# A convolution with max pooling: first quarter loaded as fp32, cleared tiles on GpSimd, a new order of all instructions

## The chip, the cores and the metric

One core of a Trainium2 chip runs the kernel. The metric is the device time of one execution in microseconds; before the change its median is 99.69 us over three runs (99.55 to 99.73).

## The reference

```python
x_pad = np.pad(x, ((0, 0), (0, 0), (1, 1), (1, 1)))
conv[b, co] += weight[co, ci, kh, kw] * x_pad[b, ci, kh:kh+h, kw:kw+w]   # over ci, kh, kw
output[b, c, i, j] = np.max(conv[b, c, 2*i:2*i+2, 2*j:2*j+2])
```

`x` is 16 x 64 x 64 x 64 and `weight` 128 x 64 x 3 x 3, both fp32; the output is 16 x 128 x 32 x 32. So it is a 3x3 convolution with padding 1 and a 2x2 maximum.

## The kernel before

**Tiling.** Two images of 64 channels fill the 128 partitions: eight pairs p. A pair is cut into four quarters q of 16 image rows, that is R = 8 output rows of 64 columns before column pooling. Such a quarter is a *step*; there are 32, numbered in the order of `SEQ`, and steps 0, 1, 2, 3 are the quarters of pair 0. Lane l (0 or 1) is one image of the pair. A matmul of a step uses 64 partitions of one lane, contracts the channels and writes 128 output channels x 512 (8 rows x 64) into one PSUM bank; matmuls of the two row halves of the array run side by side. Three matmuls (kw = 1, 0, 2) make a *product*.

**The arithmetic in the rows.** For an output pair of rows, with input rows r0 to r3 and kernel rows g0, g1, g2, a W step keeps four row tiles: E = r1 - r2, S = r1 + r2, and V, which holds both r2 - r0 (Ve) and r3 - r1 (Vo). Its products are P2 (block GM on E), P0 (G0 on V), P3 (G2 on V) and P1 (GP on S), with GM and GP half of g0 + g2 -/+ g1. A K step multiplies input rows themselves: PAa (D2 = g2 - g1), PAb (G0), PBa (D0 = g0 - g1), PBb (G2), and PR (G1 on the tile KS = r1 + r2). Step 0 is a K step, step 1 a W step. In step 0 each product but PR is cut into parts a and b of four rows: `PAb.0.1b` is step 0, lane 1, part b.

**The weights.** SP loads `wraw` (L182). DVE, ACT and POOL form the blocks G0, G1, G2, D0, D2, then GM and GP from `gsum` (tokens `c.g0`, `c.D2`, `c.GS` and so on, L211 to L231); PE transposes a block (three transposes, token T, L252), and ACT or DVE copies it from PSUM to `wt` (token TV, L263 and L267).

**The input.** SP loads the first 9 rows of pair 0 as fp32 into `first` (L184), and the tokens XO and XE cast its odd and even rows into `rows_x` (L214). All other rows come by GpSimd's DMA queue with a cast to bf16 under way (`load`, L180), in the order of `LOADS`; the first `EARLY` = 3 are issued ahead of everything else, the others at their LH tokens. DVE clears `zeros` and the top and bottom edge rows of `rows_x` (L190, L191). `make_identity` builds `ident` on POOL. Eight matmuls on constants run first on PE (L466).

**After the products.** ACT copies A's bank out (EV) and copies A into B's bank as a seed (SE, L415); DVE takes the row maximum into the bank (MX, L427), then the column maximum, alone (RM, L436) or with ACT's copy of the odd columns (OD, L431; CM, L448). SP stores (ST, ST2).

**The order.** `ORDER` is a hand-kept list of tokens, executed from left to right; the suffix names the engine (v DVE, a ACT, g POOL) or the PSUM bank. Each engine runs its own tokens in that order, and semaphores connect them. A row operation on POOL also waits for DVE's last row operation or cast ahead of it in the list (`behind`):

```python
def row_op(e, out, in0, in1, op):
    inst = eng[e].tensor_tensor(out=out, in0=in0, in1=in1, op=op)
    if e == "g":
        behind(inst, last_row[0])
    else:
        last_row[0] = inst
```

Of the kernel before, what the change touches and what calls it, by code (L numbers as in the profile page):

```python
# [17 lines left out]
XO.0a:v T.D0:4 XE.0a:a PAa.0.0a:0 PAa.0.1a:5 c.GS:g PAa.0.0a PAa.0.1a PAa.0.0a PAa.0.1a TV.D0:v PAb.0.0a  # L18
PAb.0.1a PAb.0.0a PAb.0.1a PAb.0.0a PAb.0.1a TV.G2:v PAa.0.0b PAa.0.1b PAa.0.0b PAa.0.1b LH.8 PAa.0.0b
PAa.0.1b c.GM:v PAb.0.0b PAb.0.1b PAb.0.0b PAb.0.1b PAb.0.0b PAb.0.1b PBa.0.0a:2 PBa.0.1a:4 PBa.0.0a  # L20
PBa.0.1a KS.0:v EV.0.1 PBa.0.0a PBa.0.1a PBb.0.0a PBa.0.1b PBb.0.0a PBa.0.1b TV.G1:v PBb.0.0a PBa.0.1b
T.GM:1 EV.0.0 c.GP:v PBb.0.1a PBa.0.0b PBb.0.1a PBa.0.0b PBb.0.1a PBa.0.0b TV.GM:a PBb.0.1b PBb.0.0b LH.9
E.1:v PBb.0.1b PBb.0.0b PBb.0.1b PBb.0.0b T.GP:0 P2.1.1:3 P2.1.0:1 MX.0.0 S.1:g TV.GP:a P2.1.1 P2.1.0 P2.1.1
P2.1.0 MX.0.1 PR.0.0 SE.1.1:5 PAa.2.1:0 PR.0.0 LH.10 PAa.2.1 PR.0.0 V.1:v SE.1.0:6 PAa.2.1 PAa.2.0:7 PR.0.1
PAa.2.0 RM.0.0 PR.0.1 PAa.2.0 PR.0.1 PAb.2.0 P0.1.1 PAb.2.0 E.3:v OD.0.1 P0.1.1 PAb.2.0 P0.1.1 P0.1.0 CM.0.1
P3.1.1 P0.1.0 EV.1.1 P3.1.1 P0.1.0 V.3:v P3.1.1 P3.1.0 P2.3.1:4 P3.1.0 EV.1.0 P2.3.1 P3.1.0 MX.1.1 KS.2:g
P2.3.1 P2.3.0:3 EV.2.0 PAb.2.1 P2.3.0 PAb.2.1 MX.1.0 P2.3.0 PAb.2.1 PBa.2.0:1 P1.1.1 SE.3.0:7 PBa.2.0 Ve.4:v
P1.1.1 PBa.2.0 P1.1.1 PBb.2.0 S.3:v EV.2.1 PBa.2.1:2 PBb.2.0 E2.4:v PBa.2.1 PBb.2.0 OD.1.1 PBa.2.1 P1.1.0
SE.3.1:0 PBb.2.1 P1.1.0 CM.1.1 PBb.2.1 P1.1.0 Vo.4:g PBb.2.1 P0.3.0 MX.2.0 P0.3.1 OD.1.0 P0.3.0 P0.3.1
P0.3.0 CM.1.0 P0.3.1 P3.3.0 P3.3.1 EV.3.0 P3.3.0 MX.2.1 S2.4:g ST2.1 P3.3.1 P3.3.0 P3.3.1 PR.2.0 EV.3.1  # L30
P2.4.1:6 PR.2.0 MX.3.0 P2.4.1 PR.2.0 P2.4.1 P2.4.0:3 PR.2.1 OD.2.0 P2.4.0 MX.3.1 PR.2.1 P2.4.0 PR.2.1 P1.3.0
CM.2.0 PAa.6.1:5 P1.3.0 PAa.6.1 KS.6:g P1.3.0 RM.2.1 PAa.6.1 PAa.7.0:1 P1.3.1 OD.3.0 PAa.7.0 P1.3.1 PAa.7.0
SE.4.0:4 CM.3.0 P1.3.1 PAb.7.0 PAb.6.1 PAb.7.0 LH.11 V.5:v OD.3.1 PAb.6.1 PAb.7.0 PAb.6.1 P0.4.0 SE.4.1:7
PAa.7.1:2 P0.4.0 CM.3.1 PAa.7.1 P0.4.0 PAa.7.1 P3.4.0 ST2.3 V2.8:v P0.4.1 EV.4.0 P3.4.0 P0.4.1 P3.4.0 P0.4.1
P2.5.0:0 EV.7.0 P3.4.1 P2.5.0 P3.4.1 P2.5.0 EV.4.1 MX.4.0 P3.4.1 PAa.6.0:3 E.8:g PAb.7.1 PAa.6.0 SE.5.0:1
PAb.7.1 PAa.6.0 MX.4.1 PAb.7.1 PAb.6.0 PBa.7.1:6 PAb.6.0 EV.7.1 PBa.7.1 PAb.6.0 S2.8:v LH.12 PBa.7.1 P1.4.0
P1.4.1 P1.4.0 EV.6.0 V2.10:v P1.4.1 P1.4.0 P1.4.1 PBa.6.0:2 PBb.7.1 OD.4.0 PBa.6.0 PBb.7.1 PBa.6.0 OD.4.1
# [515 lines left out]
```

## Time and profile before

| | |
|---|---|
| median of three runs | 99.69 us |
| the profiled execution | 99.57 us, span 97.8 us |
| TensorE clock granted | 0.996 |
| first product of step 0 | 5.55 us |
| step 1 begins on PE | 9.38 us |
| PE busy | 92.4 us, 845 matmuls |
| DVE busy | 88.9 us |
| ACT busy | 82.9 us |
| POOL busy | 68.4 us |

Times within the profile count from the span's start. A row of a timeline gives the start, the duration, engine, line, operation, out<-in with partitions x elements, how many instructions are merged, and in brackets the idle time ahead with what ended it. PE is matmuls, PEld weight loads, DVE VectorE, ACT ScalarE, POOL GpSimd, SP the engine that issues most stores. Landing is the time from a DMA's issue to its completion.

### The profile page before, as it was taken

The page shows a single profiled execution, that of the slowest core. Times are in us where ns is not written, and L with a number is a line of the kernel's source. Part 1 is how long each engine was busy: PE and PEld are TensorE (multiplying, and loading weights), DVE is VectorE, ACT ScalarE, POOL GpSimd, SP SyncE. Part 2 cuts the span into 40 slices and gives each one's busy share as a digit, 9 for nine tenths or more (in the row PEclk, how much of TensorE's full clock was granted, in tenths as well). Part 3 has the DMA queues.
Part 4 walks back from the last instruction along what each step waited for, and adds up shares of the span by engine and source line. Part 5 has one row for each costly group of instructions (what it writes and reads, how often), then busy time and mean ns, then how long its engine had stood idle before and what let it go on. Part 6 is the DMA issues. An engine that isn't in the chain of part 4 may idle for free.

```text
span 97.8 us, 2315 instructions
## 1 busy us (share of the span) xinstructions
PE 92.4 (94%) x845; PEld 57.6 (59%) x845; DVE 88.9 (91%) x172; ACT 82.9 (85%) x177; POOL 68.4 (70%) x60
## 2 busy tenths in 40 slices
PE   6998999999999999999999999999999999999920
PEld 2394554555886885666667555564555557777600
DVE  3459999999999999999999999999998999997960
ACT  5466688599779999999999999999989999889830
POOL 5994545936488867989584876759499779599200
PEclk9999999999999999999999999999999999999998
DMA  2999999999999999999999740405050503254052
GB/s 55 237 145 196 169 204 216 218 233 230 250 225 244 225 245 330 238 227 299 225 230 291 285 144 27 188 3 189 32 214 0 217 4 137 84 214 144 17 188 80
DMA packets 7675, 17.36 MB, mean 178 GB/s; under 512 B 624, under 2 KB 2544, under 8 KB 7024
## 3 DMA queue, kind: packets, MB, share of 16 engines
q0 software_dynamic: 2160, 8.24, 43.3%
q1 hardware_dynamic: 5216, 8.72, 25.6%
q10 hardware_dynamic: 288, 0.26, 0.8%
q8 instruction: 6, 0.10, 0.4%
q14 instruction: 5, 0.04, 0.1%
HBM read 17.07 MB, written 8.39 MB: 260 GB/s over the span
## 4 chain that ended last, share of the span: by engine, by line
PE 83%; POOL 5%; DVE 4%; issue 3%; ACT 1%; ACTq 0%; POOLq 0%
PE acc L369 82%; POOL rows_x L180 4%; DVE o L448 2%; DVE acc L427 1%; POOL gsum L219 1%; ACT acc L415 1%; PE acc L252 1%; DVE wq L219 1%; ACT ev L401 1%; POOL ident masks.py:199 0%; POOL ident masks.py:197 0%; ACTq L415 0%; POOLq L534 0%
## 5 line engine op out<-in xcount | busy, mean ns | idle before, releaser
L369 PEld LDWEIGHTS <-wt 64*128 64x128 bf16 x816 | 55.2, 94 | 31.2 <-issue 1.8
L369 PE MATMUL acc<-wv,wt 64*128 64x504 bf16 (+1 forms) x264 | 49.9, 377 | 0.0
L427 DVE TENSOR_TENSOR acc<-acc,ev 128x512 f32<-128x512 f32 x64 | 42.7, 689 | 1.2 <-ACT acc L415 0.5
L369 PE MATMUL acc<-ws,wt 64*128 64x512 bf16 (+1 forms) x168 | 40.8, 376 | 0.0
L369 PE MATMUL acc<-we,wt 64*128 64x512 bf16 (+1 forms) x168 | 39.3, 377 | 0.0
L401 ACT ACTIVATE ev<-acc 128x512 f32<-128x512 f32 x56 | 32.7, 605 | 1.8 <-PE acc L369 1.7
L415 ACT COPY acc<-acc 128x512 f32<-128x512 f32 x56 | 32.2, 590 | 2.1 <-PE acc L369 1.3
L219 POOL TENSOR_TENSOR ws<-rows_x 128x512 bf16<-128x512 bf16 (+1 forms) x12 | 17.6, 1477 | 4.2 <-DVE wv L219 1.9
L431 ACT COPY od<-acc 128x256 f32<-128x256 f32 x49 | 18.0, 379 | 2.8 <-PE acc L369 2.3
L219 POOL TENSOR_TENSOR we<-rows_x 128x512 bf16<-128x512 bf16 (+1 forms) x10 | 15.4, 1542 | 6.3 <-DVE wv L219 3.8
L448 DVE TENSOR_TENSOR o<-acc,od 128x256 f32<-128x256 f32 (+1 forms) x48 | 19.1, 420 | 0.1
L369 PE MATMUL acc<-rows_x,wt 64*128 64x504 bf16 (+7 forms) x120 | 16.5, 332 | 0.0
L219 POOL TENSOR_TENSOR wv<-rows_x 128x1024 bf16<-128x1024 bf16 (+1 forms) x6 | 14.7, 2449 | 2.3 <-DVE ws L219 1.6
L369 PE MATMUL acc<-vh,wt 64*128 64x504 bf16 (+1 forms) x72 | 16.0, 377 | 0.0
L219 POOL TENSOR_TENSOR vh<-rows_x 128x512 bf16<-128x512 bf16 x8 | 9.2, 1155 | 5.6 <-DVE we L219 3.1
L436 DVE TENSOR_REDUCE o<-acc 128x256 f32<-128x512 f32 x15 | 10.2, 680 | 0.0
L180 POOL DMA_DIRECT2D rows_x<-in_x_dram x15 | 8.6, 575 | 2.1 <-DMA rows_x<-in_x_dram 1.3
L219 DVE TENSOR_TENSOR wv<-rows_x 128x1024 bf16<-128x1024 bf16 (+1 forms) x11 | 9.8, 891 | 0.0
L369 PE MATMUL acc<-ks,wt 64*128 64x504 bf16 (+1 forms) x24 | 6.0, 376 | 0.0
L403 ACT COPY ev<-acc 128x512 f32<-128x512 f32 x8 | 4.5, 586 | 0.9 <-PE acc L369 0.9
L219 DVE TENSOR_TENSOR we<-rows_x 128x1024 bf16<-128x1024 bf16 (+1 forms) x9 | 5.1, 564 | 0.0
L219 DVE TENSOR_TENSOR ws<-rows_x 128x512 bf16<-128x512 bf16 (+1 forms) x8 | 4.7, 588 | 0.0
(26 smaller groups left out, 24.1 us busy)
## 6 DMA issues: line engine op xcount, KB each, us to landing
out_dram<-o SPq DMA_DIRECT2D x13, 512.0 KB, 6.5
rows_x<-in_x_dram POOLq DMA_DIRECT2D x5, 1024.0 KB, 13.5
rows_x<-in_x_dram POOLq DMA_DIRECT2D x4, 256.0 KB, 8.4
out_dram<-o SPq DMA_DIRECT2D x3, 256.0 KB, 2.9
rows_x<-in_x_dram POOLq DMA_DIRECT2D x1, 528.0 KB, 11.9
out_dram<-o SPq DMA_DIRECT2D x4, 128.0 KB, 2.0
rows_x<-in_x_dram POOLq DMA_DIRECT2D x1, 496.0 KB, 12.7
rows_x<-in_x_dram POOLq DMA_DIRECT2D x2, 240.0 KB, 9.1
```

What stands on the lines that cost most here:

```text
L180: nc.gpsimd.dma_start(out=xs[p][:, lo + 1 : hi + 1, :], in_=rows_of(p, lo, hi))
L219: inst = eng[e].tensor_tensor(out=out, in0=in0, in1=in1, op=op)
L252: nc.tensor.transpose(tp[:, (j - lo) * 128 : (j - lo + 1) * 128], wq[:, BLOCKS[m]].rearrange("a i j c -> a (i j c)")[:, (j - lo) * CI : (j ...
L369: yield lambda kw=kw, o0=o0, o1=o1, c0=c0, c1=c1: nc.tensor.matmul(acc[t][:, i0:i1, o0:o1], wt[l * CI : l * CI + CI, K * BLOCKS[block] + T ...
L401: nc.scalar.mul(t, acc[bank["A", s, l]], -1.0)
L403: nc.scalar.copy(out=t, in_=acc[bank["A", s, l]])
L415: nc.scalar.copy(out=acc[b], in_=acc[bank["A", s, l]])
L427: nc.vector.tensor_tensor(out=t, in0=t, in1=lanes(ev[s], l), op=MAX)
L431: nc.scalar.copy(out=t[:, l], in_=sums(s, l)[..., 1::2])
L436: nc.vector.tensor_reduce(out=lanes(outs(s), l), in_=pairs, axis=mybir.AxisListType.X, op=MAX,)
L448: nc.vector.tensor_tensor(out=t, in0=a[..., 0::2], in1=u, op=MAX)
```

## The change

`first` now holds the whole first quarter with one row more (17 rows), in two transfers from SP; the load of rows 9 to 16 by GpSimd's queue is gone, and no load is issued ahead of `make_identity`. The two clears go from DVE to POOL. In step 0 the products of the plain blocks, PAb and PBb, open the PSUM groups instead of PAa and PBa (`TAPS_FIRST`). XO and XE exist for both parts now. `ORDER` is new from the first token to the last. (The file also gains two functions, `sums_begin` and `sums_end`, that no token of the new list calls.)

```diff
-LOADS = ((0, 9, 17), (0, 17, 33), (0, 33, 49), (0, 49, 64), (1, 0, 17), ...
-EARLY = 3
+LOADS = ((0, 17, 33), (0, 33, 49), (0, 49, 64), (1, 0, 17), ...
+EARLY = 0
+TAPS_FIRST = 1
 ORDER = """
-LH.3 LH.4 c.g0:a c.D2:v LH.5 c.g2:v c.g1:a T.D2:0 T.G0:1 LH.6 c.D0:v TV.D2:a T.G2:2 T.G1:3 TV.G0:a LH.7
+LH.0 c.g0:a c.g2:v c.D2:g c.g1:v T.G2:0 c.D0:v T.G0:1 TV.G2:a T.G1:2 LH.1 T.D2:3 XE.0a:a TV.G0:v LH.2 T.D0:0
...
-    first = const.tile([128, R + 1, W], FP32, name="first")
-    nc.sync.dma_start(out=first, in_=rows_of(0, 0, R + 1))
+    first = const.tile([128, 2 * R + 1, W], FP32, name="first")
+    for lo, hi in ((0, R + 1), (R + 1, 2 * R + 1)):
+        nc.sync.dma_start(out=first[:, lo:hi], in_=rows_of(0, lo, hi))
...
-    nc.vector.memset(zeros, 0.0)
-    nc.vector.memset(rows_x[:, :, 0 : H + 2 : H + 1, :], 0.0)
+    nc.gpsimd.memset(zeros, 0.0)
+    nc.gpsimd.memset(rows_x[:, :, 0 : H + 2 : H + 1, :], 0.0)
...
-    def to_bf16(odd, e):
-        cast(e, xs[0][:, 1 + odd : R + 2 : 2, :], first[:, odd : R + 1 : 2, :])
+    def to_bf16(odd, part, e):
+        lo, hi = (0, R + 1) if part == "a" else (R + 1, 2 * R + 1)
+        lo += (lo + odd) % 2
+        cast(e, xs[0][:, lo + 1 : hi + 1 : 2, :], first[:, lo:hi:2, :])
...
-            return block, i0, i1, rows, first and part != "b"
+            return block, i0, i1, rows, first != (TAPS_FIRST and s == 0) and part != "b"
```

How the order moves three engines at the start. POOL from its branch on, before: three loads, `ident`, five loads, gsum.

```order
L180 DMA rows_x<-in_x_dram 128x512
L180 DMA rows_x<-in_x_dram 128x1024 x2
masks.py:197 MEMSET ident 128x128
masks.py:199 ISA
masks.py:199 AFFINE_SELECT ident<-ident 128x128 [waits Pool_49]
L180 DMA rows_x<-in_x_dram 128x960
L180 DMA rows_x<-in_x_dram 128x1088
L180 DMA rows_x<-in_x_dram 128x1024 x2
L180 DMA rows_x<-in_x_dram 128x960
L219 TENSOR_TENSOR gsum<-wraw 128x192 [waits DMAHW0_49,DVE_49]
```

The same place now, where the operation that writes `wq` is D2:

```order
masks.py:197 MEMSET ident 128x128
masks.py:199 ISA
masks.py:199 AFFINE_SELECT ident<-ident 128x128 [waits Pool_49]
L192 MEMSET zeros 128x512
L193 MEMSET rows_x 128x8x2x64
L181 DMA rows_x<-in_x_dram 128x1024
L223 TENSOR_TENSOR wq<-wraw 128x256 [waits DMAHW0_49,DVE_49]
L181 DMA rows_x<-in_x_dram 128x1024
L181 DMA rows_x<-in_x_dram 128x960
L181 DMA rows_x<-in_x_dram 128x1088
```

All loads have moved behind `ident` and the clears, and all but one behind D2, which itself waits for the weights and for a cast on DVE.

DVE from its branch to E.1, before: the clears, D2, the cast of g2, D0, the cast XO, two copies of transposed blocks, GM, KS, a copy, GP, E.1.

```order
L190 MEMSET zeros 128x256
L191 MEMSET rows_x 128x8x2x32
L219 TENSOR_TENSOR wq<-wraw 128x256 [waits DMAHW0_49]
L212 CAST wq<-wraw 128x256
L219 TENSOR_TENSOR wq<-wraw 128x256
L212 CAST rows_x<-first 128x4x64 [waits DMAHW1_49]
L267 COPY wt<-acc 128x384 [waits PE_49]
L267 COPY wt<-acc 128x384
L219 TENSOR_TENSOR wq<-gsum,wraw 128x256 [waits Pool_49]
L219 TENSOR_TENSOR ks<-rows_x 128x512 [waits DMASW0_49,DVE_49,Activation_49]
```

Now: the casts of g2 and g1, D0, the copy TV.G0, gsum, the cast XO of part b, GM, GP, KS, E.1.

```order
L214 CAST wq<-wraw 128x256 [waits DMAHW0_49]
L214 CAST wq<-wraw 128x256
L223 TENSOR_TENSOR wq<-wraw 128x256
L271 COPY wt<-acc 128x384 [waits PE_49]
L223 TENSOR_TENSOR gsum<-wraw 128x192
L214 CAST rows_x<-first 128x4x64 [waits DMAHW2_49]
L223 TENSOR_TENSOR wq<-gsum,wraw 128x256 [waits DVE_49]
L223 TENSOR_TENSOR wq<-gsum,wraw 128x256
L223 TENSOR_TENSOR ks<-rows_x 128x512 [waits DVE_49,Activation_49]
L223 TENSOR_TENSOR we<-rows_x 128x512 [waits DMASW0_49]
```

gsum came to DVE, D2 left it, GM no longer waits for POOL, and KS no longer waits for a load; E.1 (`we`) is the first that does.

PE's transposes of D2 and D0 and the first product, now:

```order
L256 LDWEIGHTS wq [waits Pool_49]
L256 MATMUL acc<-ident,wq 128x128
L256 LDWEIGHTS wq
L256 MATMUL acc<-ident,wq 128x128
L256 LDWEIGHTS wq
L256 MATMUL acc<-ident,wq 128x128
L256 LDWEIGHTS wq [waits DVE_49]
L256 MATMUL acc<-ident,wq 128x128 [waits Activation_49]
...
L383 LDWEIGHTS wt
L383 MATMUL acc<-rows_x,wt 128x256 [waits Activation_49]
```

D2's transposes wait for POOL where they waited for DVE, and they stand fourth of the five blocks where they stood first.

More of the change, by code (lines that the diff above doesn't have):

```diff
@@ L18 @@
[L18 to L37, printed above, removed]
@@ new lines @@
+PAb.0.1b PAb.0.0b PAa.0.1b PAb.0.0b c.GP:v PAa.0.1b PAa.0.1b T.GM:3 LH.5 PAa.0.1a PBa.0.0a KS.0:v PAa.0.1a
+PBa.0.0a PAa.0.1a PBa.0.0a TV.GM:a PBb.0.1b PAa.0.0a LH.6 PBb.0.1b PAa.0.0a PBb.0.1b PAa.0.0a TV.G1:a
+PBa.0.1b PBb.0.0b PBa.0.1b PBb.0.0b PBa.0.1b PBb.0.0b LH.7 EV.0.1 PBa.0.1a PAa.0.0b PBa.0.1a PAa.0.0b E.1:v
+PBa.0.1a PAa.0.0b T.GP:2 EV.0.0 P2.1.0:0 P2.1.1:7 MX.0.1 P2.1.0 P2.1.1 TV.GP:a P2.1.0 P2.1.1 V.1:v PBa.0.0b
+PBa.0.0b PR.0.1 SE.1.0:1 PBa.0.0b PR.0.1 PAa.2.0:2 PR.0.1 PAa.2.0 MX.0.0 SE.1.1:6 S.1:g PAa.2.1:3 PAa.2.0
@@ new lines @@
+PAa.2.1 P0.1.0 RM.0.1 PAa.2.1 P0.1.0 P0.1.1 P0.1.0 P0.1.1 P3.1.0 E.3:v EV.1.0 LH.8 P0.1.1 P3.1.0 P3.1.1
+P3.1.0 V.3:v P3.1.1 PR.0.0 EV.1.1 LH.9 P3.1.1 PR.0.0 PAb.2.1 PR.0.0 MX.1.0 S.3:g PAb.2.1 P2.3.0:0 OD.0.0
+PAb.2.1 P2.3.0 P2.3.1:7 P2.3.0 CM.0.0 EV.2.1 P2.3.1 P1.1.0 P2.3.1 P1.1.0 MX.1.1 PBa.2.1:5 P1.1.0 KS.2:g
+SE.3.0:4 PBa.2.1 PAb.2.0 PBa.2.1 PAb.2.0 RM.1.0 SE.3.1:3 PBb.2.1 PAb.2.0 PBb.2.1 P0.3.0 EV.2.0 PBb.2.1
+P0.3.0 E2.4:v P1.1.1 P0.3.0 P1.1.1 PBa.2.0:1 EV.3.0 P1.1.1 PBa.2.0 V2.4:v P0.3.1 PBa.2.0 P0.3.1 P2.4.0:2
@@ new lines @@
+PAa.6.0 P1.4.1 PAa.6.0 PAa.7.1:2 CM.3.2 P2.5.0:1 OD.4.1 PAa.7.1 E.9:g P2.5.0 PAa.7.1 P2.5.0 PAb.6.1 CM.4.2
+ST2.3 PAb.6.0 PAb.6.1 SE.5.0:3 PAb.6.0 PAb.6.1 PAb.6.0 PAb.7.1 V2.8:v LH.11 PBa.6.0:6 PAb.7.1 EV.6.0 PBa.6.0
+PAb.7.1 PBa.6.0 P2.5.1:4 PBb.6.0 EV.7.1 P2.5.1 PBb.6.0 P2.5.1 V2.10:v PBb.6.0 PBa.6.1:5 P0.5.0 SE.5.1:2
+PBa.6.1 P0.5.0 PBa.6.1 P0.5.0 PBb.6.1 EV.6.1 P3.5.0 PBb.6.1 E.8:v P3.5.0 PBb.6.1 EV.5.0 P3.5.0 P0.5.1
+E2.10:v PAa.7.0:0 P0.5.1 PAa.7.0 P0.5.1 PAa.7.0 MX.6.2 P3.5.1 S2.10:g P2.8.0:1 EV.5.1 P3.5.1 P2.8.0 P3.5.1
@@ L306, in two_quarters, with sums_begin, sums_end @@
         row[name, s], row[name, place.index((p, q + 1))] = t[:, 0:half], t[:, half:]
+    def sums_begin(p, e):
+        eng[e].dma_start(out=xs[p - B // 2 + 2][:, 1:H], in_=xs[p][:, 1:H])
+    def sums_end(p, h):
+        lo, hi = 1 + h * H // 2, H // 2 + h * H // 2
+        t = xs[p - B // 2 + 2]
+        nc.gpsimd.dma_start(out=t[:, lo:hi], in_=xs[p][:, lo + 1 : hi + 1], accum_op=ADD)
+        for q in (2 * h, 2 * h + 1):
+            row["S", place.index((p, q))] = t[:, 2 * R * q + 1 : 2 * R * q + 2 * R : 2]
     def all_rows(s, e):
```

159 lines of the change are left out of this document (84 added, 75 removed).

## The prediction

> **What bounds the kernel now.** I read the page's first part, then the table by stages, then what the weight loads of TensorE wait for. First the page's engine totals.
>
> ```profile
> span 97.8 us, 2315 instructions
> PE 92.4 (94%) x845; PEld 57.6 (59%) x845; DVE 88.9 (91%) x172; ACT 82.9 (85%) x177; POOL 68.4 (70%) x60
> ```
>
> The table by stages has PE, PEld, DVE, ACT and POOL busy time in each stretch.
>
> ```profile
> 9.38:20.00 10.62, 10.62 (x100) 5.33 (x101) 10.56 (x21) 7.94 (x17) 7.29 (x8) 1.00 1.10 202
> ...
> 40.00:50.00 10.00, 10.00 (x96) 6.88 (x93) 9.95 (x21) 9.84 (x21) 7.95 (x7) 1.00 1.05 246
> 50.00:60.00 10.00, 10.00 (x95) 6.00 (x92) 9.99 (x22) 9.97 (x25) 6.73 (x5) 1.00 0.66 206
> ```
>
> From 9.38 us on PE never rests, and DVE rests 0.06 us of 10.62 and 0.01 to 0.05 of 10: two engines are full at once, and ACT nearly so in the middle. So the later part is a balance in which little can be won, and the change has to earn its time before 9.38 us, or by taking away what PE still waits for. Those waits, from 5 to 92 us (total, times, longest):
>
> ```profile
> PEld L252 <- DVE wq L219: 0.8, 2, 0.5
> PEld L369 <- DVE o L448: 0.8, 3, 0.3
> PEld L369 <- DVE acc L427: 0.6, 2, 0.3
> ```
>
> The first is the start: the transposes of the weight blocks GM and GP come late. The other two, 1.4 us, are PE waiting for a PSUM bank that DVE has not emptied. The start itself, from the timelines of DVE, POOL and PE:
>
> ```profile
> 3.75 0.61 DVE L219 TENSOR_TENSOR wq<-wraw 128x256 bf16<-128x256 f32 x1 [2.07 <-DMA wraw<-in_weight_dram]
> 4.28 0.38 DVE L212 CAST wq<-wraw 128x256 bf16<-128x256 f32 x1
> 4.58 0.62 DVE L219 TENSOR_TENSOR wq<-wraw 128x256 bf16<-128x256 f32 x1
> 5.10 0.33 DVE L212 CAST rows_x<-first 128x256 bf16<-128x256 f32 x1
> 6.36 0.85 POOL L219 TENSOR_TENSOR gsum<-wraw 128x192 f32<-128x192 f32 x1
> 7.24 0.62 DVE L219 TENSOR_TENSOR wq<-gsum,wraw 128x256 bf16<-128x256 f32 x1 [0.96 <-POOL gsum L219]
> 8.11 0.35 DVE L267 COPY wt<-acc 128x384 bf16<-128x384 bf16 x1
> 8.91 0.41 DVE L219 TENSOR_TENSOR we<-rows_x 128x512 bf16<-128x512 bf16 x1
> 4.42 1.20 PE L252 MATMUL acc<-ident,wq 128*128 128x128 bf16 x15
> 5.55 2.11 PE L369 MATMUL acc<-rows_x,wt 64*128 64x256 bf16 x36
> 7.92 0.34 PE L252 MATMUL acc<-ident,wq 128*128 128x128 bf16 x3 [0.25 <-DVE wq L219]
> 8.19 0.83 PE L369 MATMUL acc<-rows_x,wt 64*128 64x256 bf16 x12
> 9.05 0.34 PE L252 MATMUL acc<-ident,wq 128*128 128x128 bf16 x3
> 9.38 0.39 PE L369 MATMUL acc<-we,wt 64*128 64x512 bf16 x2
> ```
>
> Weights land, five blocks are transposed, step 0's first product starts at 5.55, and step 1 (the `we` products, P2.1) starts at 9.38. I forecast the shift of that last moment and of E.1, the DVE operation at 8.91 that feeds it.
>
> **The change part by part.** *First product.* D2 moves to POOL and waits there for DVE's cast of g2, now first on DVE: 3.75 + 0.38 + some 0.07 for the signal = 4.2. The nearest POOL row, gsum, took 0.85 us for 192 fp32 elements, so 256 take 1.13; DVE's own row for the operation is 0.61. I take 1.13: D2 ends at 5.33, not 4.36. Meanwhile D0, a subtraction of two SBUF operands on DVE, wants to start at about 4.4. What such a pair does to each other the trace shows here, POOL's operation first, then DVE's two:
>
> ```profile
> 56.96 2.12 POOL L219 TENSOR_TENSOR wv<-rows_x 128x1024 bf16<-128x1024 bf16 x1 [0.76 <-DVE ws L219]
> 58.76 0.60 DVE L219 TENSOR_TENSOR ws<-rows_x 128x512 bf16<-128x512 bf16 x1
> 59.29 0.41 DVE L219 TENSOR_TENSOR vh<-rows_x 128x512 bf16<-128x512 bf16 x1
> ```
>
> POOL reads until 59.08. The DVE operation that started at 58.76 took 0.60, an equal one behind it 0.41: it stood still for 0.19, to 0.13 before POOL's end. So D0 starts at 5.2 in effect and ends at 5.82. [...]
>
> PE then has T.D2 and T.D0 in front of the first product, whichever block that product needs; fifteen transposes took 1.20, so T.D0's three end 0.24 after D0, and the first product starts at about **6.1, 0.55 late**. If D2 took only 0.61, D0 would end at 5.3 and the shift would be 0; if D0 were not blocked, T.D2 and T.D0 would follow D2's end at 5.33, and the product would start at 5.85.
>
> *From there to P2.1.* Half-size products run as pairs on the two row halves: six pairs in 0.83, less the last one's drain, is 0.11 a pair. Before P2.1 stand three singles, nine pairs, T.GM, twelve pairs, T.GP: 12 x 0.11 = 1.32 to 7.42; a transposed block takes 0.27 (7.92 to 8.19), to 7.69; 1.32 to 9.01; T.GP 0.33 (9.05 to 9.38): **9.34, where it was 9.38**. The two waits for GM and GP are gone, because gsum is now made on DVE behind D0 and TV.G0 (5.82 + 0.35, then 0.62 x 192/256 = 0.47, less an overlap of 0.1 between rows: 6.5, where POOL gave it at 7.21 behind eight DMA issues). A cast (0.33) and GM (0.62) follow, so GM is ready near 7.3, just before T.GM's 7.42. But three halves (PBa.0.0b) are left for after P2.1, about half of 3 x 0.11 = 0.16 of PE time. So PE stands **0.12 worse** than before; with D0 unblocked it stands 0.13 better, with D2 at 0.61 it stands 0.43 better.
>
> *Casts and copies.* The second half of the quarter needs two more casts and ACT takes TV.D2, TV.D0, TV.G1 and one cast from DVE.
>
> ```profile
> 4.96 0.86 ACT L263 COPY wt<-acc 128x384 bf16<-128x384 bf16 x2
> 5.70 0.47 ACT L211 CAST rows_x<-first 128x320 bf16<-128x320 f32 x1
> ```
>
> ACT's list from 5.0 (TV.G2 done) is three casts and two copies, 3 x 0.47 + 2 x 0.43 = 2.3, so TV.D0 is ready at 7.3, 0.4 before its product at 7.69: hidden. Without that cover it would cost what it is late. SP issues the second half of `first` behind the first half, and nothing else waits on SP.
>
> *GpSimd and the loads.* POOL now makes `ident`, clears `zeros` and the edge rows, and only then issues the load of rows 17 to 32, which E.1 needs. The rows on what these take:
>
> ```profile
> 0.86 0.27 DVE L190 MEMSET zeros<- 128x256 uint32 x1 [0.86 <-PEq L534]
> 1.19 0.48 DVE L191 MEMSET rows_x<- 128x512 uint32 x1
> 2.97 0.23 POOL masks.py:197 MEMSET ident<- 128x128 bf16 x1
> 3.28 0.29 POOL masks.py:199 TENSOR_SCALAR_AFFINE_SELECT ident<-ident 128x128 bf16<-128x128 bf16 x1
> 1.24 0.70 POOL L180 DMA_DIRECT2D rows_x<-in_x_dram  x1 [0.79 <-POOLq L534]
> 1.93 0.53 POOL L180 DMA_DIRECT2D rows_x<-in_x_dram  x1
> ```
>
> `ident` takes 0.6 (2.97 to 3.57). The clears lie between DVE's 0.75 and, at the 0.23 / 128 = 1.8 ns an element of POOL's only memset, 1536 x 1.8 = 2.8; part of that 0.23 is fixed, so I take 1.8. [...] With a start at 0.9 the load is issued near 3.3 (2.2 to 4.3), where it was 1.93. How long it flies, from the answers on DMA (landing times, then the queues in 1.2 to 3.5, 3.5 to 4.5 and 7 to 8.5 us):
>
> ```profile
> rows_x<-in_x_dram POOLq DMA_DIRECT2D x1, 128.0 KB, 4.9
> rows_x<-in_x_dram POOLq DMA_DIRECT2D x1, 256.0 KB, 6.8
> ```
> ```profile
> q1 hardware_dynamic: 229, 0.48, 67.3%
> ```
> ```profile
> q0 software_dynamic: 91, 0.09, 63.6%
> ```
> ```profile
> q0 software_dynamic: 163, 0.29, 108.6%
> ```
>
> POOL's queue moves nothing until 3.5, 2.3 after the first issue, so packets start at 3.3 + 2.3 = 5.6. At 0.29 MB in 1.5 us, 256 KB take 1.36: 7.0 at the earliest. But the first 128 KB landed at 1.24 + 4.9 = 6.1, 1.9 later than that rate allows, and the second load at 1.93 + 6.8 = 8.7, 3.2 later. With a lag of 0 to 3.2 the load lands between 7.0 and 10.2; I take 8.6, since two loads shared the larger lag. P2.1 at 9.34 needs E.1 started by 8.85, so this just fits, and E.1 starts at 8.65 instead of 8.91: **DVE is 0.26 ahead**. The later loads queue behind one another and land 1.4 apart; rows 33 to 48 come at 10.0, and PE asks for them a microsecond after P2.1.
>
> *The rest of the order.* PE runs the same products. DVE's list from E.1 on has six operations fewer, and the differing shapes cancel to within one maximum:
>
> ```profile
> L427 DVE TENSOR_TENSOR acc<-acc,ev 128x512 f32<-128x512 f32 x64 | 42.7, 689 | 1.2 <-ACT acc L415 0.5 <-ACT ev L401 0.2 <-PE acc L369 0.2
> ```
>
> I put it at 0, with bounds of 0.69 either way. What the lead is worth: each of the five bank waits (1.4 us together, 0.3 at most) shortens if DVE arrives earlier. A lead of 0.26 can return up to that at the first wait after which PE pulls up; I take 0.3 with what the removed overheads give, bounds 0 and 1.4.
>
> Sum: +0.12 - 0.3 = **-0.2** against this execution. Its own time is 99.57 (the span of 97.8 and 1.8 around it), 0.12 under the median of 99.69, so I forecast 99.37 + 0.12 = **99.5**.
>
> **The rivals.** *Late load (slower).* The transfer decides as soon as it lands after 8.8. If it lags like the first two loads did, at 9.5, E.1 runs at 9.55, PE starts P2.1 at 10.0 and DVE is behind by 0.6: +0.6 to +0.8, **100.4**. For it: issue is 1.4 later than before, and the lag was there twice. Against: 128 KB less stand ahead in the queue, and the hardware queue, which shared the engines at 4, is finished.
>
> *More won.* POOL's subtraction is short or does not block D0, the load lands near 7.5, DVE is a microsecond ahead and most bank waits go: -0.13 to -0.43 at PE and -0.4 of waits, **99.0**. For it: 1.4 us of waits are there. Against: the 0.19 us standstill quoted above.
>
> *It does not do what it says.* The start gains nothing and the new order of the later part has its own bank waits, one or two of 0.3 more: **100.0**. For it: three engines are full, and a few tenths decide; against: the same counts of work.
>
> **How the numbers follow.** Forecast 99.5 (99.2 to 99.75) 0.42; late load 0.25; more won 0.18; order worse 0.15. The range is 98.9 to 100.5, from the middle of the second to that of the first rival. 0.2%, 0.2 us, is about what a measurement can tell from no change. Faster by more: 0.21 of the forecast's share and all of the third, 0.39. Within: 0.17 + 0.05 = 0.22. Slower: 0.04 + 0.25 + 0.10 = 0.39.
>
> **What would show it.** D0's DVE row should last about 1.4 us where it was 0.62; the first product should start near 6.1, T.GM without a wait near 7.4, P2.1 near 9.3. E.1 should be released by the load's landing at 8.4 to 8.8. Wrong would be a clear that takes over 2.5 us, a landing before 8 or after 9, or a bank-wait total over 2 us between 10 and 90.

## The result, and the profile after

The change makes the kernel **slower**: 101.03 us in the median of four executions (100.89 to 102.18) against 99.65 for the kernel before (99.55 to 99.73), a ratio of 1.0163 with a 95% interval of 1.0127 to 1.02. The forecast was 99.5, with a range that ended at 100.5. The profiled execution is the slowest of the four, 102.18 us with a span of 100.4. A second set of ten executions (experiment 12) has a median of 100.94, ratio 1.0117 (1.0087 to 1.0148), and gave a second profile. The ratios leave out executions that took over 1.5% longer than the fastest one of the same kernel.

The engine totals after, from the page:

```profile
span 100.4 us, 2314 instructions
PE 93.8 (93%) x845; PEld 58.2 (58%) x845; DVE 89.0 (89%) x163; ACT 83.7 (83%) x178; POOL 69.8 (70%) x59
```

The table by stages after; the third row begins at TensorE's matmul number 174.

```profile
9.29:20.00 10.71, 9.19 (x82) 4.54 (x81) 8.23 (x14) 7.02 (x15) 4.97 (x6) 1.00 1.09 193
20.00:30.00 10.00, 10.00 (x93) 6.12 (x91) 10.00 (x16) 7.98 (x18) 7.00 (x7) 1.00 1.06 237
22.37:92.37 70.00, 70.00 (x645) 45.45 (x643) 69.04 (x128) 65.26 (x141) 53.83 (x36) 1.00 0.65 179
```

The first of these stretches in the kernel before, and its 70 us from the same matmul on.

```profile
9.29:20.00 10.71, 10.71 (x101) 5.39 (x101) 10.65 (x22) 7.94 (x17) 7.38 (x8) 1.00 1.10 202
...
19.77:89.77 70.00, 70.00 (x646) 45.59 (x643) 69.06 (x130) 66.21 (x144) 53.00 (x37) 1.00 0.68 186
```

Read the matmul counts. From 9.29 to 20 us TensorE gets 82 matmuls done where it did 101; over the 70 us that follow, 645 where it did 646. So the loss lies wholly in the first steps, and the new order of the later part is neither better nor worse. Counting matmuls in the traces says where exactly. The table gives the time at which TensorE starts its matmul number n in the kernel before, and by how much the others are later there (845 is the last matmul of all, 78 stands about at the start of step 1; the expectations below count products, so that their 144th is number 174 here). The last column is the time of the profiled execution itself, not the median:

| n | 30 | 78 | 126 | 174 | 845 | profiled execution, us |
|---|---|---|---|---|---|---|
| before (us) | 5.89 | 9.38 | 14.57 | 19.77 | 93.16 | 99.57 |
| after | +0.35 | +0.14 | +1.02 | +2.60 | +2.56 | 102.18 |
| after, second profile (12) | +0.46 | +0.24 | +1.71 | +1.69 | +1.70 | 101.30 |
| 1 clears on DVE | +0.59 | +1.65 | +1.56 | +1.55 | +1.56 | 101.16 |
| 3 loads later | +0.33 | +0.55 | +2.87 | +2.89 | +2.88 | 102.49 |
| 4 loads ahead, clears and D2 on DVE | +0.17 | +3.29 | +3.20 | +3.18 | +3.21 | 102.79 |
| 5 loads ahead, D2 on DVE | +0.23 | -0.05 | -0.14 | -0.16 | -0.14 | 99.48 |
| 6 two loads ahead | +0.71 | +0.50 | +0.41 | +0.39 | +0.42 | 100.00 |
| 10 one load ahead | +0.42 | +0.21 | +0.70 | +0.73 | +0.73 | 100.32 |

Whatever TensorE is behind at matmul 174 it is behind at the end, to within 0.04 us, in every row, and in the profiles of experiments 2, 7, 9 and 11 too. What it waited for after, DVE's and TensorE's rows of the timeline:

```profile
4.23 1.42 DVE L223 TENSOR_TENSOR wq<-wraw 128x256 bf16<-128x256 f32 x1
7.83 0.42 DVE L223 TENSOR_TENSOR we<-rows_x 128x512 bf16<-128x512 bf16 x1
12.80 0.42 DVE L223 TENSOR_TENSOR we<-rows_x 128x512 bf16<-128x512 bf16 x1 [0.70 <-DMA rows_x<-in_x_dram]
17.59 0.69 DVE L223 TENSOR_TENSOR we<-rows_x 128x1024 bf16<-128x1024 bf16 x1 [1.54 <-DMA rows_x<-in_x_dram]
5.97 1.42 PE L383 MATMUL acc<-rows_x,wt 64*128 64x256 bf16 x21
9.29 0.82 PE L383 MATMUL acc<-we,wt 64*128 64x512 bf16 x6
10.97 0.39 PE L383 MATMUL acc<-rows_x,wt 64*128 64x512 bf16 x1 [0.43 <-DMA rows_x<-in_x_dram]
18.34 0.39 PE L383 MATMUL acc<-we,wt 64*128 64x512 bf16 x1 [0.99 <-DVE we L223]
```

The start is as forecast: D0 took 1.42 us, the first product starts at 5.97, step 1 at 9.29, and E.1 at 7.83 had its load already. Then three transfers come late: rows 33 to 48 of pair 0 (TensorE idle 0.43 at 10.97), rows 49 to 63 (DVE idle 0.70 at 12.80) and rows 17 to 32 of pair 1 (DVE idle 1.54 at 17.59, TensorE 0.99 behind it). GpSimd's rows say why, with the landing times of four loads (LH.0, LH.1, LH.2, LH.4) from the answers on DMA behind them:

```profile
1.25 0.53 POOL L192 MEMSET zeros<- 128x512 bf16 x1
1.72 0.95 POOL L193 MEMSET rows_x<- 128x1024 bf16 x1
2.61 0.70 POOL L181 DMA_DIRECT2D rows_x<-in_x_dram  x1
4.11 1.06 POOL L223 TENSOR_TENSOR wq<-wraw 128x256 bf16<-128x256 f32 x1 [0.80 <-DVE wq L214]
5.09 3.75 POOL L181 DMA_DIRECT2D rows_x<-in_x_dram  x7
```
```profile
rows_x<-in_x_dram POOLq DMA_DIRECT2D x1, 256.0 KB, 4.8
```
```profile
rows_x<-in_x_dram POOLq DMA_DIRECT2D x1, 256.0 KB, 5.8
rows_x<-in_x_dram POOLq DMA_DIRECT2D x1, 240.0 KB, 7.0
```
```profile
rows_x<-in_x_dram POOLq DMA_DIRECT2D x1, 256.0 KB, 10.8
```

LH.0 is issued at 2.61 and lands after 4.8, at 7.45; the next load is issued only at 5.09, behind D2, and lands at 10.93, LH.2 at 12.7, LH.4 (issued at 6.70) at 17.5. In between the transfer engines move half of what they moved before at that time. The stretch from 6 to 8 us after (the last two columns are the transfer engines' busy share and GB/s):

```profile
6.00:8.00 2.00, 2.00 (x33) 1.62 (x34) 2.00 (x6) 1.22 (x4) 2.00 (x5) 1.00 0.74 88
```

and before:

```profile
6.00:8.00 2.00, 1.75 (x34) 1.44 (x29) 1.04 (x4) 1.13 (x3) 1.68 (x3) 1.00 1.02 180
```

88 GB/s against 180 over 2 us is 184 KB that were not moved. An estimate: at the 193 to 202 GB/s of the stage that follows they take 0.9 us to catch up, and in that stage the engines' busy share is 1.09 to 1.10 already.

### The profile page after: what moved, and what is told of

It is laid out like the page before. It is cut to its first block, busy times and chain, and to the rows that moved or that the text cites. A ratio compares the mean times of both kernels' runs of the same rounds, so it can differ in the third digit from the quotient of the medians.

```text
span 100.4 us, 2314 instructions
## 1 busy us (share of the span) xinstructions
PE 93.8 (93%) x845; PEld 58.2 (58%) x845; DVE 89.0 (89%) x163; ACT 83.7 (83%) x178; POOL 69.8 (70%) x59
## 4 chain that ended last, share of the span: by engine, by line
PE 76%; DMA 14%; DVE 3%; POOL 3%; DVEq 0%; issue 0%
PE acc L383 76%; DMA rows_x<-in_x_dram 11%; DMA wraw<-in_weight_dram 3%; POOL rows_x L181 2%; DVE o L462 1%; POOL wq L223 1%; DVE we L223 1%; DVE acc L441 1%; DVE wq L214 0%; DVEq L566 0%; DVEq L223 0%
## 5 line engine op out<-in xcount | busy, mean ns | idle before, releaser
L383 PE MATMUL acc<-wv,wt 64*128 64x504 bf16 (+1 forms) x312 | 62.4, 377 | 0.0
L441 DVE TENSOR_TENSOR acc<-acc,ev 128x512 f32<-128x512 f32 (+1 forms) x61 | 42.6, 718 | 1.5 <-PE acc L383 1.1
L383 PE MATMUL acc<-ws,wt 64*128 64x512 bf16 (+1 forms) x168 | 40.0, 376 | 0.1
L223 POOL TENSOR_TENSOR ws<-rows_x 128x1024 bf16<-128x1024 bf16 (+1 forms) x13 | 21.7, 1672 | 13.6 <-DVE we L223 5.5
L223 POOL TENSOR_TENSOR wv<-rows_x 128x1024 bf16<-128x1024 bf16 (+1 forms) x9 | 21.0, 2342 | 5.3 <-DVE wv L223 1.7
L383 PE MATMUL acc<-rows_x,wt 64*128 64x504 bf16 (+5 forms) x120 | 17.2, 331 | 0.4 <-DMA rows_x<-in_x_dram 0.4
L223 POOL TENSOR_TENSOR we<-rows_x 128x512 bf16<-128x512 bf16 (+1 forms) x9 | 11.3, 1260 | 3.5 <-DVE wv L223 2.6
L223 DVE TENSOR_TENSOR we<-rows_x 128x1024 bf16<-128x1024 bf16 (+1 forms) x11 | 6.5, 602 | 2.2 <-DMA rows_x<-in_x_dram 2.2
L383 PE MATMUL acc<-vh,wt 64*128 64x504 bf16 (+1 forms) x24 | 5.8, 377 | 0.0
L480 PE MATMUL acc<-const-bfloat16-1.0 128*128 128x512 bf16 x8 | 3.6, 628 | 0.8 <-PEq L552 0.8
## 6 DMA issues: line engine op xcount, KB each, us to landing
rows_x<-in_x_dram POOLq DMA_DIRECT2D x1, 496.0 KB, 12.7
```

Source lines behind the costliest of these rows:

```text
L383: yield lambda kw=kw, o0=o0, o1=o1, c0=c0, c1=c1: nc.tensor.matmul(acc[t][:, i0:i1, o0:o1], wt[l * CI : l * CI + CI, K * BLOCKS[block] + T ...
L441: nc.vector.tensor_tensor(out=t, in0=t, in1=lanes(ev[s], l), op=MAX)
L480: nc.tensor.matmul(acc[n], ones[:, 0:128], ones, start=True, stop=True, skip_group_check=True)
```

## The experiments

Theory A: the loads that the change put behind D2 on GpSimd land late, and that is the loss. The first rival: the new order of steps 0 to 4 costs by itself. The second came up on the way: the fp32 half of the first quarter and the loads stand in one another's way.

**1. The clears back on DVE.**

```diff
-    nc.gpsimd.memset(zeros, 0.0)
-    nc.gpsimd.memset(rows_x[:, :, 0 : H + 2 : H + 1, :], 0.0)
+    nc.vector.memset(zeros, 0.0)
+    nc.vector.memset(rows_x[:, :, 0 : H + 2 : H + 1, :], 0.0)
```

> The changed kernel with its two clears back on DVE. The load of rows 17 to 32 is then issued near 1.3 us instead of 2.61, all others still behind D2 at 5.1. Theory 'loads behind D2': the first load had 0.4 us to spare already, rows 33 to 48 land at 10.5 to 11 as before, PE still waits for them and for pair 1, so the time stays within 0.4 of 101.0. Rival 'clears delay everything': with the clears gone the time returns to 99.6 to 99.8.

101.17 us (100.82 to 102.7), ratio 1.0147 (1.0115 to 1.0178): no gain, and the loss is in another place: it stands at +1.65 by the start of step 1 and grows no more. So the time came as the first theory expected, but not for its reason. The transfers of the first quarter from SP, in the changed kernel and here, and the DVE row that waits:

```profile
first<-in_x_dram SPq DMA_DIRECT2D x1, 256.0 KB, 3.4
```
```profile
first<-in_x_dram SPq DMA_DIRECT2D x1, 256.0 KB, 6.1
```
```profile
7.74 0.29 DVE L214 CAST rows_x<-first 128x256 bf16<-128x256 f32 x1 [1.32 <-DMA first<-in_x_dram]
```

Now LH.0 is issued at 1.43, before the second half of `first` (1.64), and that half takes 6.1 us where it took 3.4. So the clears on GpSimd were no mere cost: with them the first load was issued at 2.61, and the half landed at 5.04 and not at 7.74.

**2. The clears on DVE, and four loads ahead of D2.**

```diff
-LH.0 c.g0:a c.g2:v c.D2:g c.g1:v T.G2:0 c.D0:v T.G0:1 TV.G2:a T.G1:2 LH.1 T.D2:3 ...
+LH.0 c.g0:a c.g2:v LH.1 LH.2 LH.3 LH.4 c.D2:g c.g1:v T.G2:0 c.D0:v T.G0:1 TV.G2:a T.G1:2 T.D2:3 ...
```

> As the run before, and the next four loads (rows 33 to 63 of pair 0, rows 0 to 32 of pair 1) stand ahead of D2 on GpSimd, issued between 1.3 and 4.1 us. Nothing else is moved. Theory 'loads behind D2': they land near 9.6, 10.9, 12.5 and 13.8, PE waits for none, matmul 144 comes at 19.8 to 20.0 as in the kernel before (22.4 in the changed one), and the time is 99.7 (99.4 to 99.9). Rival 'new order': steps 1 to 4 wait for something else than loads, and the time stays over 100.5.

100.6 to 100.9 us in three executions and 104.5 to 104.6 in three others. The loads land as in the kernel before (LH.1 at 9.8, LH.4 at 13.7), and still nothing is won, since the half of `first` takes 6.7 us. So neither theory had this wait. In the profile (104.59 us) TensorE then runs at half its clock for 6.8 us (page, a digit for each fortieth of the span):

```profile
PEclk9995569999999999999999999999999999999999
```

**3. The loads spaced.** Four clears of `zeros` (2.3 us) stand between LH.1 and LH.2; nothing else is changed.

```diff
-... LH.1 T.D2:3 XE.0a:a TV.G0:v LH.2 T.D0:0
+... LH.1 T.D2:3 XE.0a:a TV.G0:v ZP.4 LH.2 T.D0:0
```

> The changed kernel with four clears of the unread tile zeros (2.1 us) on GpSimd between the second load (rows 33 to 48, issued at 5.1) and the third. It asks why the second load took 5.8 us to land. Theory 'burst': issuing seven loads in a row slows the packets in flight; alone, the second load lands at 9.6 or earlier. Rival 'fixed flight': it lands at 10.6 to 11.0 all the same. The later loads come 2.1 us later and the time rises by 1 to 2 us in both.

102.49 us in its one execution. LH.1 lands at 9.98 instead of 10.93: without loads right behind it it flies 4.9 us and not 5.8. LH.2, issued 2.27 later, lands at 14.56 instead of 12.71, and TensorE loses its time there: the row at 15.13 has 1.52 us of idle time behind DVE's E.3. Here a load that is issued later moves the loss with it and makes it larger.

```profile
15.13 0.39 PE L382 MATMUL acc<-we,wt 64*128 64x512 bf16 x1 [1.52 <-DVE we L222]
```

**4. Experiment 2 with D2 on DVE as well** (`c.D2:v` behind the loads).

> As the second run (clears on DVE, loads ahead), and D2 back on DVE right after the cast of g2, so that no GpSimd operation reads SBUF while D0 runs. Theory 'lock': D0 lasts 0.62 instead of 1.42 us, ends 0.3 earlier in spite of D2 in front of it, step 1 starts on PE near 9.0 instead of 9.3, and the time is 0.2 to 0.3 under the second run. Rival: the first product is set by ACT's copies and casts; no change against the second run.

99.49, 101.96, 102.52 and 102.79 us. D0 lasts 0.61 us, as was expected without GpSimd's subtraction beside it. The half of `first` takes 6.2 us in the profiled execution (102.79), and TensorE's clock falls again, for 3.4 us. One execution, at 99.49 and without a profile, suggests what is possible when neither happens.

**5. As 4, but the clears on GpSimd**, so that the loads start at 2.61.

```diff
-LH.0 c.g0:a c.g2:v c.D2:g c.g1:v T.G2:0 ...
+LH.0 c.g0:a c.g2:v LH.1 LH.2 LH.3 LH.4 c.D2:v c.g1:v T.G2:0 ...
```

> The clears stay on GpSimd, D2 goes back to DVE, and the loads LH.1 to LH.4 are issued right behind LH.0, from 2.6 us on. Theory A (the loads that the change put behind D2 land late, and nothing else costs): the second half of the fp32 quarter still lands by 5.3, because GpSimd's packets start only some 2 us after the first issue; LH.1 to LH.4 land near 9.2, 10.6, 12.0 and 13.5; the first product starts near 5.6; TensorE at its 144th product matmul is within 0.4 us of the kernel before; 99.0 to 99.6 us. Theory B (the new order of steps 0 to 4 costs by itself): the loads land like that and it still takes 100.5 or more. Theory C (the fp32 half and the loads share the transfer engines, so that one of them is always late): the half lands at 7 or later, TensorE idles 1 to 2 us there, 101 to 102.8.

99.51 us (99.33 to 99.9, ten executions), ratio 1.0 (0.9985 to 1.0015): the whole loss is gone, with the new order of everything else in place. The half of `first` takes 3.8 us and lands at 5.41; the loads land at 8.27, 9.57, 11.43, 13.2 and 14.45. The stretch from 6 to 8 us, then two TensorE rows:

```profile
6.00:8.00 2.00, 2.00 (x36) 1.60 (x33) 1.73 (x5) 1.40 (x5) 1.16 (x3) 1.00 1.04 174
```
```profile
5.78 1.42 PE L382 MATMUL acc<-rows_x,wt 64*128 64x256 bf16 x21
9.10 0.82 PE L382 MATMUL acc<-we,wt 64*128 64x512 bf16 x6
```

Theory A holds and the order as a rival falls: with the loads in time and D2 on DVE, the new order is as fast as the kernel before. What the loads do alone, with D2 left on GpSimd, is experiment 10.

**6. Only LH.1 and LH.2 ahead of D2**, which stays on GpSimd.

```diff
-LH.0 c.g0:a c.g2:v c.D2:g c.g1:v T.G2:0 ...
+LH.0 c.g0:a c.g2:v LH.1 LH.2 c.D2:g c.g1:v T.G2:0 ...
```

> Only LH.1 and LH.2 move ahead of D2 on GpSimd; D2 stays there and starts some 0.25 us later (4.4 instead of 4.11). Theory A: the half of the fp32 quarter by 5.3, LH.1 near 9.2, LH.2 near 10.6, LH.4 near 14, nothing waits for a load for over 0.2; the first product near 6.2; 99.5 to 100.1 us. Theory B: 100.6 or more without a wait for a load. Theory C: the fp32 half lands at 7 or later, 101 to 102.8.

100.00 us (99.9 to 100.12), ratio 1.0043 (1.0029 to 1.0057). No load is waited for. What is left against experiment 5, 0.49 us, is D2 on GpSimd: it lasts from 4.53 to 5.51, D0 beside it takes 1.69 us instead of 0.62 and ends only at 6.00, and the first product starts at 6.33 instead of 5.78.

```profile
4.53 0.98 POOL L222 TENSOR_TENSOR wq<-wraw 128x256 bf16<-128x256 f32 x1
```
```profile
4.31 1.69 DVE L222 TENSOR_TENSOR wq<-wraw 128x256 bf16<-128x256 f32 x1
```

**7. The kernel before, with late loads.**

```diff
-LH.3 LH.4 c.g0:a c.D2:v LH.5 c.g2:v ... LH.6 ... LH.7 ... LH.8 ... LH.9 ... S.1:g TV.GP:a
+LH.3 LH.4 c.g0:a c.D2:v c.g2:v ... S.1:g LH.5 LH.6 LH.7 LH.8 LH.9 TV.GP:a
```

> The kernel before, with its loads LH.5 to LH.9 (pair 1 from row 17 on, and pair 2) moved behind S.1 on GpSimd, so that the load of rows 17 to 32 of pair 1 is issued at 9.5 to 10.7 us where it was at 4.77. Theory A: it lands at 15.5 to 17.2; DVE wants those rows at 14.9 and waits 0.6 to 2.3; the whole comes out as much later: 100.2 to 101.8 us. Theory B: a wait of that kind is made good further on, 99.4 to 99.8.

99.9 us (99.39 to 100.48), ratio 1.0024 (0.9999 to 1.005): inconclusive. Issued at 10.57, behind a queue that was busy for 52.8% of the time from 10.6 to 10.8, LH.5 flew only 4.6 us and landed at 15.18, earlier than expected. So it does not decide between the theories. The +0.52 at the end of its profile reads as another cause: GpSimd's KS.2, moved by the issues to 13.75, ran beside DVE's Ve.4, which took 0.98 instead of 0.41.

```profile
13.75 1.21 POOL L219 TENSOR_TENSOR ks<-rows_x 128x512 bf16<-128x512 bf16 x1
```
```profile
14.27 0.98 DVE L219 TENSOR_TENSOR vh<-rows_x 128x512 bf16<-128x512 bf16 x1
```

**8. Experiment 4 with five matmuls on constants** where TensorE waits for the half of `first`.

```diff
-... PBb.0.0a PAb.0.1b PBb.0.0a ...
+... PBb.0.0a F.7.5 PAb.0.1b PBb.0.0a ...
```

> The kernel of experiment four (clears and D2 on DVE, loads ahead), with five matmuls on constants (1.1 us at full clock) put ahead of the first product that needs the second half of the fp32 quarter. They compute nothing that is used. Clock theory (the long idle of TensorE there makes the granted clock fall to a half, and that is what spreads the executions from 99.5 to 102.8): the idle that is left is under 0.9 us, the clock stays at 1.00, and all executions lie within 1 us of one another, between 100.3 and 101.4. Rival (the late landing alone costs, the clock follows from something else): the clock falls again or the spread stays at 2 to 3 us, with executions above 102.

101.11 to 101.95 us in four executions. The half landed late again (8.53), the idle left was 1.08 us and not under 0.9, and the time is above what was expected; but in the profile the clock stayed at 1.00, and the executions lie within 0.84 us, where experiment 4's span 3.3. So the late half explains a loss of some 2 us here. That the fall of the clock is what came on top of it in the profiles of experiments 2 and 4 fits its length there, 6.8 and 3.4 us at half speed, but rests on these profiles alone.

**9. Experiment 5 with the transposes of D2 and D0 behind the first two matmuls of the first plain product, and those of GP earlier.**

```diff
-T.G1:2 T.D2:3 XE.0a:a TV.G0:v T.D0:0 XO.0a:a c.GS:v PBb.0.1a:4 PBb.0.1a TV.D2:a ... T.GP:2 EV.0.0
+T.G1:2 XE.0a:a TV.G0:v XO.0a:a c.GS:v PBb.0.1a:4 PBb.0.1a T.D2:3 T.D0:0 TV.D2:a ... EV.0.0
```

> Experiment five's kernel, with the transposes of D2 and D0 moved behind the first two matmuls of the first plain product, and the transposes of GP moved six products earlier, ahead of E.1 in the list. A shift of TensorE's start has so far come out at the end one to one. Theory A (TensorE's start still has idle time in it: 0.19 us before T.D0, 0.21 before T.GM and 0.21 before T.GP in experiment five's profile, and taking it away is worth as much at the end, as long as E.1 has its load): the first product starts at 5.4 to 5.6 instead of 5.78, T.GP waits for nothing, step 1 begins at 8.8 to 8.95 instead of 9.10; 99.15 to 99.4 us. Rival (the landing of rows 17 to 32 near 8.3 with E.1 behind it, or DVE as the other full engine, holds step 1 and what follows): 99.45 to 99.65, no difference.

100.13 us (99.91 to 100.56), ratio 1.0057 (1.0038 to 1.0076): worse. The first product did start earlier, at 5.52, but two single matmuls and six transposes then filled 0.75 us up to 6.27, and step 1 began at 9.37. The idle time ahead of the transposes was not to be had that way.

**10. The changed kernel with one token moved**, LH.1 ahead of D2.

```diff
-LH.0 c.g0:a c.g2:v c.D2:g c.g1:v ... T.G1:2 LH.1 T.D2:3 ...
+LH.0 c.g0:a c.g2:v LH.1 c.D2:g c.g1:v ... T.G1:2 T.D2:3 ...
```

> The changed kernel with one token moved: the load LH.1 (rows 33 to 48) ahead of D2 on GpSimd, in the 0.80 us in which GpSimd waits there for DVE. Theory A (the transfer engines ran half empty between 6 and 8 us because the next load was issued 1.8 us after the first had been): LH.1 lands at 9.2 to 9.6 instead of 10.93, LH.2 near 11.5, LH.4 before 15; at 6 to 8 us 120 to 180 GB/s flow instead of 88; D2 and the first product stay where they were (4.1 and 6.0); 99.8 to 100.3 us. Rival (only the loads behind D2 count, one moved load changes little): LH.3 and LH.4 land as late as before, 100.7 to 101.2.

99.81 us (99.7 to 101.08, ten executions), ratio 1.0034 (1.0007 to 1.0061): one load, issued in the time in which GpSimd waits for DVE anyway, takes back 1.2 of the 1.4 us. LH.1 lands at 9.17, and from 6 to 8 us the transfer engines move 191 GB/s instead of 88:

```profile
6.00:8.00 2.00, 2.00 (x32) 1.59 (x32) 2.00 (x6) 1.07 (x4) 2.00 (x5) 1.00 1.09 191
```

In its profile (100.32 us, one of the slower executions) LH.2 still comes late, at 12.39, and DVE waits 0.59 for it.

**11. Experiment 4 with two more clears on GpSimd ahead of the first load** (`ZP.2 LH.0`).

> Experiment four's kernel (clears and D2 on DVE, loads ahead), with GpSimd clearing the tile `zeros` twice more ahead of the first load, for no use but time: 1.06 us by the 0.53 that one such clear takes there. Theory A (it is the time of the first load's issue, 1.43 or 2.6, that decides whether the second half of the fp32 quarter is delayed, whoever makes the clears): the first load is issued at 2.3 to 2.7, the half lands by 5.6, TensorE does not idle for over 0.4 us between 6 and 9, the clock is 1.00 there, and all executions lie between 99.2 and 100.0 us. Rival (the clears' place itself, or chance, makes experiment four's executions slow): executions above 101.5 and the half at 7 or later, as before.

100.26 us (99.48 to 100.84), ratio 1.0056 (1.0017 to 1.0096). The clears took less than expected, the load was issued at 2.31, and the half of `first` landed at 7.17 in the profile: 5.5 us of flight against 6.2 in experiment 4 and 3.4 to 3.8 with an issue at 2.61. Three of ten executions were at 99.5. This is a mixed answer: a later issue shortens the flight of the half, as expected, but at 2.31 it still lands as late as the rival said. In the profile the clock did not fall, and nothing lies above 100.84.

**12. The changed kernel once more.**

> The changed kernel unaltered, for a second profile, since the first one was its slowest execution. Theory A: the load of rows 17 to 32 of pair 1 lands at 16.3 to 17.6 and the loads of rows 33 to 48 and 49 to 63 of pair 0 at 10.5 to 11 and 12.5 to 13; what TensorE is behind the kernel before at its 144th product matmul is within 0.2 us of what the whole is behind; 100.8 to 101.4 us in most executions. Rival (those landings were that execution's own): they come 0.8 us or more sooner and the loss sits elsewhere.

100.94 us (100.33 to 101.3, ten executions). In this profile (101.3 us) most of the loss is one wait of 1.28 us: LH.1, issued at 5.06, landed after 6.8 us at 11.88, LH.4 at 16.1 in time.

```profile
11.93 0.39 PE L383 MATMUL acc<-rows_x,wt 64*128 64x512 bf16 x1 [1.28 <-DMA rows_x<-in_x_dram]
```

All three landings missed what was expected, by 0.2 to 0.9 us, but TensorE's delay is still that of the whole: it is 1.69 behind at matmul 174, and 101.3 - 99.57 is 1.73. Which load costs most differs between the two profiles; in both it is one that stands behind D2.

## Why the prediction was wrong

*First product and step 1: right.* D0 was to last 1.4 us and took 1.42, the first product was to come at 6.1 and came at 5.97, step 1 at 9.34 and came at 9.29, TensorE was to be 0.12 behind and was 0.14. The clears were put at 1.8 us and took 1.4 (1.25 to 2.67): 0.53 for 512 elements, 0.95 for 1024 and 0.20 for the 128 of `ident`, so some 0.1 of each does not grow with the size, an estimate from these three rows. That D0 on DVE lasts longer beside GpSimd's subtraction is shown by experiments 5 and 6: it takes 0.62 without it and 1.69 with it, and the difference of the two experiments is 0.49 us.

*The first load: too late in the forecast.* It was to land at 8.6 and landed at 7.45, issued at 2.61 instead of 3.3 and with 4.8 us of flight instead of 5.3. A landing before 8 was one of the prediction's own signs of being wrong. The rival of a late load was placed here, and here it did not come true; that it put the time at 100.4, nearer to what was measured, is luck.

*The later loads: the step that failed.* The prediction said that they land 1.4 apart, rows 33 to 48 at 10.0, and gave them no price. That sentence took over the spacing of loads that are issued back to back. But LH.1 was issued 2.5 us after LH.0, the transfer engines moved 88 GB/s from 6 to 8 us (102 in the second profile) where they had moved 180, and LH.1 landed 3.5 us behind LH.0 in the first profile and 4.1 in the second, at 10.93 and 11.88. Those behind it followed at 12.71 and 14.51 (13.21 and 14.80), 1.3 to 1.8 apart. So the spacing within the burst was about right, and the gap in front of it was missing. (That LH.4 came 3.0 us behind LH.3 in the first profile and 1.3 in the second is not explained.) LH.1, LH.2 and LH.4 carry rows that were issued before at 2.46, 3.52 and 4.77, and are issued now at 5.09, 5.66 and 6.70, that is 2.6, 2.1 and 1.9 us later. The rows of before showed how little there was to spare: the first readers of the three loads, then how long the loads flew.

```profile
10.02 0.38 PE L369 MATMUL acc<-rows_x,wt 64*128 64x512 bf16 x1
11.77 0.41 DVE L219 TENSOR_TENSOR we<-rows_x 128x512 bf16<-128x512 bf16 x1
14.90 0.68 DVE L219 TENSOR_TENSOR we<-rows_x 128x1024 bf16<-128x1024 bf16 x1
```
```profile
rows_x<-in_x_dram POOLq DMA_DIRECT2D x1, 256.0 KB, 7.5
```
```profile
rows_x<-in_x_dram POOLq DMA_DIRECT2D x1, 240.0 KB, 7.6
```
```profile
rows_x<-in_x_dram POOLq DMA_DIRECT2D x1, 256.0 KB, 9.3
```

TensorE took rows 33 to 48 at 10.02 with the load in at 9.97, E.3 at 11.77 had its rows at 11.12, and E2.4 at 14.90 had them at 14.05: a slack of 0.05, 0.65 and 0.85. Each load needed its own line of issue, flight and first reader, and only the first one got it. Price: TensorE falls back by 2.46 from matmul 78 to 174 in the first profile and by 1.45 in the second; experiment 10, which moves only the first of these loads, gives back 1.2 of the median.

*The lead of DVE, -0.3: nothing.* E.1 did run 1.1 us earlier, but DVE could not carry that on. Its next operation waited 0.94 us for TensorE and started at 9.19, where it had started at 9.24 before:

```profile
9.19 0.70 DVE L441 TENSOR_TENSOR acc<-acc,ev 128x512 f32<-128x512 f32 x1 [0.94 <-PE acc L383]
```

No bank wait was returned either. From 20 to 92 us TensorE's weight loads after wait 1.4 us for DVE, as before (0.8 + 0.6):

```profile
PEld L383 <- DVE acc L441: 0.8, 3, 0.5
PEld L383 <- DVE o L450: 0.3, 1, 0.3
PEld L383 <- DVE o L462: 0.3, 1, 0.3
```

After the late loads DVE had no lead left that could return any, so experiment 5, where TensorE waits for no load, says more. There E.1 ran 0.61 earlier than before, E.3 0.21 and E2.4 0.08; the waits were 1.0 us; and TensorE was 0.05 to 0.16 ahead from step 1 on, and no more than that at the end. The waits are those of weight loads: in the 70 us of the tables above TensorE's matmul rows, whose ends are modelled, show no idle time, before or after, that a lead could have taken away. So the rival of a greater gain, 99.0, had nothing to draw on.

*The sum* put right: +0.14 for the start, +1.2 for the late loads by experiment 10, 0 for the lead: +1.3, against +1.4 measured. The rival that the new order is bad by itself falls with experiment 5.

## What to carry to other kernels

When loads move on their queue, write down for each of them, not for the first alone, how much later it is issued and how much slack its first reader had; here, after a pause of 2.5 us between two issues, 88 GB/s flowed from 6 to 8 us where it had been 180, and the loads behind the pause paid. This kernel, with its two main engines full, gave nothing back: what the start lost or won stood unchanged at the end. And before a cost is moved off an engine's start, look at what it held back: here, with the clears on GpSimd, the half of `first` flew 3.4 us, and 6.1 with the clears on DVE and the first load issued at 1.43.
